# The first stage of a diffusion block rebuilt: modulation on column groups of TensorE, its squares summed there, and the values of two heads at a time

## The chip, the cores and the metric

One core of one Trainium2 chip. The metric is device time in microseconds (us), the median of three runs of the whole program. The core has five engines that run side by side, each in the order of its own program: TensorE (PE in the rows; PEld is its weight load), VectorE (DVE), ScalarE (ACT), GpSimd (POOL) and SyncE (SP), which here mostly issues transfers. Semaphores order one engine after another.

## The reference, cut to what matters

One block of a diffusion backbone, on 128 context tokens and 1024 latent tokens of 1024 features. What the change touches is the very beginning:

```
sh1, sc1, ... = silu(cond) @ w_mod + b_mod            # cond: one vector for the context, one for the sample
h   = x * rsqrt(mean(x*x) + eps) * g_norm_mix * (1 + sc1) + sh1    # 1152 tokens x 1024 features
z   = h @ w_in                                        # latents, q, k, v (1024 columns), gates, branches
```

Behind it come an attention over compressed latents, a bidirectional mLSTM (4 heads, values of 256 columns a head), gates, an output projection and a feed-forward part. All products are done in float32 accuracy.

## The kernel before, in words

Tokens lie along the free dimension and features on the 128 partitions: x^T is 8 row blocks (k = 0 to 7) of 128 features by 1152 tokens, handled in two halves of 576 tokens. Each operand of a large product is split into a high part (`hi`, ScalarE, L69) and a low part (`lo`, VectorE, L75: the difference), and a product is three matmuls, L98 (hi, hi), L99 (hi, lo) and L100 (lo, hi).

`start` (L329) is the first stage. Its steps:

- Transfers, in the order of SyncE's queue: two blocks of the modulation's matrix (`wm`, 1 MB each), the first half of x (four transfers, 2.36 MB), the first weights of the values (`wr`, 0.5 MB), the second half of x, then four more `wm` blocks and further weights.
- `gemv(b)` (L354): four times 128 columns of the modulation. Eight matmuls with the condition (128 rows, 2 columns) on the weight side and 512 columns of w_mod on the moving side (L356), then four small matmuls that turn the two rows into columns (L361). It is called for b = 0, 1, 2. The last two feature blocks, k = 6 and 7, are done instead as rows against a broadcast condition (`row`, L375 to L386, weights `wm3`) on VectorE, GpSimd and ScalarE.
- `stats(j)`: ScalarE squares a row block of half j, VectorE adds it to an accumulator (`sq_acc`, L156). `rows` (L259) then sums the accumulator over the partitions by five fp32 matmuls against a column of ones (L267), VectorE does rsqrt on 5 columns (L117 to L123) and five diagonal matrices `dg` (L274), TensorE broadcasts (L280) and ScalarE copies the factors to `ar` (L281).
- `xr(j)` (L423) multiplies the row blocks by the factors, k = 0 and 1 on VectorE, 2 to 7 on GpSimd. `modk(k, j)` applies scale and shift (ScalarE for the first half, VectorE L428 for the second) and splits the result into the operands B (high and low).
- The values: one head at a time (N = 256), 9 token chunks in the groups GA (6 chunks) and GB (3 chunks), each with an own PSUM bank; 4 heads x 9 chunks x 8 k x 3 = 864 matmuls. Only head 0 of group GA is multiplied while the modulation runs. A weight block (`wr`, 128 x 1024, four k of a head) is split into `wh` and `wl`, which share four buffers. `copy4` (L442, GpSimd) collects the chunk that straddles both halves; `vout` copies a finished bank to `vs` and stores it.
- `t_ops` (L543): four subtractions of 128 x 2304 elements on GpSimd (L547 and the like) that prepare operands of later products. They run beside the values.

Behind `start` comes `z_lat` (L574), whose first product is the first matmul with 288 columns. The order is that of each engine's instructions, which a scheduler settles from the code; the waits come from the buffers and from the data.

Of the kernel before, what the change touches and what calls it, by code (L numbers as in the profile page):

```python
# [19 lines left out]
P = 128  # L20
# [36 lines left out]
class K:  # L57
# [25 lines left out]
    def load_w(self, src, kt, w, bufs=None):  # L83
        """Stream one weight block [P, kt, w] from DRAM and split it exactly."""
# [27 lines left out]
    def rsqrt(self, ssq, width, n, pool):  # L112
        """1/sqrt(ssq/n + eps) on the vector engine: exponent estimate and three Newton steps."""
# [12 lines left out]
    def row_rstd(self, rbc, acc, n, pool, pp, tag, chunks=CHUNKS, more=None):  # L126
        """rbc[:, t] = 1/sqrt(sum_p (acc[p, t] + more[p, t])/n + eps) on every partition."""
# [30 lines left out]
    def modulate(self, raw, t, sc, sh, k):  # L158
        """raw = t * sc + sh with the context's and the sample's own columns."""
# [4 lines left out]
    # ------------------------------------------------------------------  # L164
# [48 lines left out]
    # vec columns  # L213
    V_GMIX, V_GFFN, V_GFIN, V_GML, V_GQ, V_GKV, V_BG = 0, 8, 16, 24, 32, 35, 37
# [24 lines left out]
    def tick(self, n=1):  # L239
        """Emit n pieces of the work that runs beside the products."""  # L240
# [18 lines left out]
    def rows(self, rbc, acc, n, pool, pp, tag):  # L259
        """rbc[:, t] = 1/sqrt(sum_p acc[p, t]/n + eps) on every partition."""  # L260
# [28 lines left out]
    def inputs(self):  # L289
        """Everything that reads the modulated input (all of w_in), the mLSTM and the attention's projections."""  # L290
# [38 lines left out]
    def start(self, vp):  # L329
        """Norm and modulation of the input, and the mLSTM's values."""  # L330
        nc, a, pp = self.nc, self.a, self.pp
        es = contextlib.ExitStack()
        sp = es.enter_context(self.pool("s1"))
        nc.scalar.dma_start(self.silc, a["cT"])
# [12 lines left out]
        def block(b):  # L347
            for i in range(2):
                w = self.slot(((8, 9), (10, 11), (5, 6))[b][i], [P, 4, 512], "wm", F32)
# [18 lines left out]
        sr = self.slot(7, [P, 2, D], "sr0", F32)  # L368
        rw = {}

        def rload(f):
            rw[f] = self.wp.tile([P, D], F32, name=self.nm("wr"), tag="wr", bufs=self.wb[0])
            nc.sync.dma_start(rw[f], a["wm3"][f])

        def row(f):  # L375
            """Shift (f even) or scale of block 6 + f // 2 of the features, as rows against the broadcast condition."""
            w = rw.pop(f)
            m = 8 * (f % 2) + 6 + f // 2
            o = self.mod1[:, m]
            for e in range(2):  # L380
                if e == 0 or f in (2, 3):
                    t = sp.tile([P, D], F32, name=self.nm("mj"), tag="mj")
                    nc.vector.scalar_tensor_tensor(t, w, 1.0, sr[:, e], op0=ALU.mult, op1=ALU.mult, accum_out=o[:, e:e + 1])
                else:
                    nc.gpsimd.tensor_tensor(w, w, sr[:, 1], op=ALU.mult)
                    nc.scalar.activation(w, w, AF.Copy, accum_out=o[:, 1:2])  # L386

        def rparams(k):
            for m in (k, 8 + k):
                nc.vector.tensor_scalar(self.mod1[:, m], self.mod1[:, m], self.bm[:, m:m + 1], None, op0=ALU.add)  # L390
            nc.vector.tensor_scalar(self.A1[:, k, :], self.mod1[:, 8 + k, :], 1.0,
                                    self.vec[:, self.V_GMIX + k:self.V_GMIX + k + 1], op0=ALU.add, op1=ALU.mult)
        nc.scalar.activation(self.silc, self.silc, AF.Silu)
        ar = self.slot(13, [P, 2, T], "ar", F32)
        acc, rbc = ar[:, 0], ar[:, 1]
        wv, vraw = {}, {}

        def vload(i):
            vraw[i] = self.wp.tile([P, 4 * DV], F32, name=self.nm("wr"), tag="wr", bufs=self.wb[0])
            nc.sync.dma_start(vraw[i], a["w_v"][i // 2][:, i % 2 * 4 * DV:(i % 2 + 1) * 4 * DV])  # L400

        def loadv(h, j):
            i = 2 * h + j
            if i not in vraw:
                vload(i)
            if i and i + 1 < 2 * HM:
                vload(i + 1)
# [1644 lines left out]
```

## Time and profile before

| | us |
|---|---|
| runs | 2242.07, 2245.0, 2249.43 |
| median | 2245.0 |
| profiled execution, its span | 2242.8 |
| TensorE busy | 2083.1 (93%) |
| VectorE busy | 1659.5 (74%) |
| GpSimd busy | 1127.2 (50%) |
| ScalarE busy | 1068.0 (48%) |

The page gives no time of the profiled execution beside its span; the span is 2.2 us under the median of the runs. The TensorE clock in the page is the share of full speed that was granted (1.0 is 2.4 GHz, 0.5 is 1.2 GHz). The first of the 40 slices of the page (56 us each) shows TensorE at 6 tenths and the second at 7, all later ones at 8 or 9: the stage that is changed is where TensorE stands idle most.

### The profile page before, as it was taken

How to read it: one execution, taken by the hardware profiler on the slowest of the kernel's cores; microseconds unless marked ns; L12 is line 12 of the kernel's file. 1: busy time of each engine (PE TensorE's matmuls, PEld its weight loads, DVE VectorE, ACT ScalarE, POOL GpSimd, SP SyncE). 2: the span in 40 equal slices, each digit the busy share in tenths (PEclk: the TensorE clock that was granted, in tenths of full speed). 3: DMA queues.
4: the chain of work that ended last, by engine and by line, in shares of the span. 5: the costliest groups of instructions: out<-in, count | busy, mean ns of one | idle time of the engine just before them, and what ended most of it. 6: DMA issues, size and time to landing. Idle time of an engine off the chain costs nothing.

```text
span 2242.8 us, 40186 instructions
## 1 busy us (share of the span) xinstructions
PE 2083.1 (93%) x14713; PEld 1998.2 (89%) x14713; DVE 1659.5 (74%) x2998; ACT 1068.0 (48%) x2225; POOL 1127.2 (50%) x850
## 2 busy tenths in 40 slices
PE   6799999999989987999999999879999999989898
PEld 2799998999978776998998999879999999989897
DVE  6725745988845879998987666899755565799895
ACT  4322333445445556777776435444322222356464
POOL 3612122667624415877877543677867634431411
PEclk8899999999999998999999999999999999999899
DMA  7121244555479775322224575223555522557664
GB/s 286 63 93 59 90 142 124 164 174 183 152 241 330 238 230 175 90 74 65 84 66 102 170 224 157 86 83 122 186 177 183 175 89 80 161 173 248 206 201 138
DMA packets 234532, 340.97 MB, mean 152 GB/s; under 512 B 18110, under 2 KB 170398, under 8 KB 233310
## 3 DMA queue, kind: packets, MB, share of 16 engines
q1 hardware_dynamic: 225790, 328.73, 46.0%
q0 software_dynamic: 4848, 6.06, 1.1%
q10 hardware_dynamic: 3696, 3.61, 0.5%
q8 instruction: 116, 1.90, 0.4%
q14 instruction: 82, 0.67, 0.1%
HBM read 250.55 MB, written 87.80 MB: 151 GB/s over the span
## 4 chain that ended last, share of the span: by engine, by line
PE 42%; DVE 16%; DMA 7%; POOL 6%; issue 6%; ACT 2%; SPq 1%; DVEq 0%; POOLq 0%; ACTq 0%
PE mm L98 10%; PE mm L100 10%; PE mm L99 10%; DVE wo L75 4%; DMA pr<-w_fo 3%; DVE sm L1374 2%; DVE pl L75 1%; PE st L98 1%; PE pv L1437 1%; PE pv L1438 1%; PE st L100 1%; PE st L99 1%; PE mx L1372 1%; DMA N<-d_nm 1%; PE p L1079 1%
## 5 line engine op out<-in xcount | busy, mean ns | idle before, releaser
L100 PE MATMUL mm<-th,wo 128*128 128x288 f32 x1840 | 546.8, 298 | 14.0 <-DVE wo L75 13.7
L98 PE MATMUL mm<-th,wo 128*128 128x288 f32 x1840 | 547.6, 298 | 2.7 <-DVE zo L1658 1.1
L99 PE MATMUL mm<-tl,wo 128*128 128x288 f32 x1840 | 546.2, 297 | 0.0
L100 PEld LDWEIGHTS mm<-th,wo 128*128 128x128 f32 x1840 | 348.9, 190 | 18.2 <-DVE wo L75 17.6
L75 DVE TENSOR_TENSOR wo<-wr,wo 128x512 fp32r<-128x512 f32 (+1 forms) x317 | 314.6, 1008 | 59.4 <-ACT wo L69 54.4
L98 PEld LDWEIGHTS mm<-th,wo 128*128 128x128 f32 x1840 | 348.2, 189 | 4.5 <-issue 1.6
L99 PEld LDWEIGHTS mm<-tl,wo 128*128 128x128 f32 x1840 | 348.3, 189 | 0.1
L69 ACT ACTIVATE wo<-wr 128x512 fp32r<-128x512 f32 (+1 forms) x317 | 187.5, 607 | 147.9 <-PE mm L100 69.5
L69 ACT ACTIVATE wo<-ws 128x512 fp32r<-128x512 f32 x188 | 116.7, 627 | 271.7 <-PE mm L100 160.5
L75 DVE TENSOR_TENSOR wo<-ws,wo 128x512 fp32r<-128x512 f32 x188 | 186.7, 996 | 62.1 <-ACT wo L69 61.9
L100 PE MATMUL mm<-xh,wo 128*128 128x288 f32 x616 | 184.7, 301 | 10.3 <-DVE wo L75 10.3
L1642 POOL TENSOR_TENSOR ws<-wr,ws 128x512 f32<-128x512 f32 x47 | 62.3, 1326 | 243.5 <-DVE wo L75 238.2
L99 PE MATMUL mm<-xl,wo 128*128 128x288 f32 x616 | 184.7, 300 | 0.0
L98 PE MATMUL mm<-xh,wo 128*128 128x288 f32 x616 | 184.2, 299 | 0.5 <-ACT wo L69 0.5
L1420 POOL TENSOR_TENSOR es<-es,p 128x512 f32<-128x512 f32 (+1 forms) x96 | 129.4, 1348 | 34.8 <-ACT p L1403 19.9
L98 PE MATMUL mm<-B,wo 128*128 128x288 f32 x456 | 134.8, 296 | 2.6 <-DVE zo L1658 1.7
L100 PE MATMUL mm<-B,wo 128*128 128x288 f32 x456 | 134.8, 296 | 0.0
L99 PE MATMUL mm<-B,wo 128*128 128x288 f32 x456 | 134.8, 296 | 0.0
L701 POOL TENSOR_TENSOR wm<-wm,sr 128x512 f32<-128x512 f32 x64 | 100.1, 1567 | 65.2 <-DVE mj L700 49.2
L100 PEld LDWEIGHTS mm<-xh,wo 128*128 128x128 f32 x616 | 118.1, 192 | 12.7 <-DVE wo L75 12.5
L98 PEld LDWEIGHTS mm<-xh,wo 128*128 128x128 f32 x616 | 118.2, 192 | 0.7 <-ACT wo L69 0.7
L99 PEld LDWEIGHTS mm<-xl,wo 128*128 128x128 f32 x616 | 118.4, 192 | 0.0
(443 smaller groups left out, 6076.6 us busy)
## 6 DMA issues: line engine op xcount, KB each, us to landing
wr<-w_ff SPq DMA_DIRECT2D x56, 512.0 KB
wm<-wm SPq DMA_DIRECT2D x32, 512.0 KB
wr<-d_w SPq DMA_DIRECT2D x32, 512.0 KB
d_z<-zo SPq DMA_DIRECT2D x48, 288.0 KB
d_g<-uu SPq DMA_DIRECT2D x44, 288.0 KB
wr<-w_big SPq DMA_DIRECT2D x24, 512.0 KB
wr<-w_fo SPq DMA_DIRECT2D x24, 512.0 KB
pr<-w_fo SPq DMA_DIRECT2D x40, 256.0 KB
```

The source lines that it names most:

```text
L69: i = self.nc.scalar.activation(out, in_, AF.Copy)
L75: return self.nc.vector.tensor_sub(out, in_, f32v(hi)).ins
L98: mm(out, lhs[0], rhs[0], start=first, stop=False)
L99: mm(out, lhs[0], rhs[1], start=False, stop=False)
L100: self.pe = mm(out, lhs[1], rhs[0], start=False, stop=last).ins
L701: nc.gpsimd.tensor_tensor(w[:, n], w[:, n], sr[:, 1], op=ALU.mult)
L1079: self.pe = mm(p1, A[:, h], V[:, h], start=True, stop=not carried).ins
L1372: nc.tensor.matmul(s[:, :kc], q[0:QK, 0, q0 + t * P:q0 + (t + 1) * P], k[0:QK, 0, k0 + j * kc:k0 + (j + 1) * kc], start=True, stop=True)
L1374: nc.vector.tensor_reduce(sm[:, 3 * t + j:3 * t + j + 1], s[:, :kc], axis=AX.X, op=ALU.max, negate=True)
L1420: G.tensor_tensor(U["sum"][:, :m], U["sum"][:, :m], p[:, :m], op=ALU.add)
L1437: nc.tensor.matmul(pv[:, :n], v[:, i], ph[:, e, :n], start=c + e == 0, stop=False)
L1642: G.tensor_tensor(s4, a12, s2, op=ALU.subtract)
```

## The change

What it does, step by step:

- Transfers: x's first half is loaded ahead of the `wm` blocks; there are eight `wm` blocks (four gemvs) instead of six, and no `wm3`.
- `gemv(b)`: the condition is padded to 32 columns, and the eight matmuls write four groups of 32 PSUM partitions in turn (k modulo 4). ScalarE copies the whole bank, and the four small matmuls, now with a selector of two columns on the moving side (L366), add the groups up. All four b are done so.
- `stats(j)`: VectorE adds nothing. Each squared row block is summed at once by five fp32 matmuls with one column (L398), which accumulate over k in PSUM: 8 x 5 = 40 for each half.
- `modk`: for k = 0 to 3 VectorE does x times scale times factor in one instruction (L421) and ScalarE adds the shift (L422); for k = 4 to 7 GpSimd multiplies by the factor (L414) and ScalarE applies scale and shift (L424), in both halves.
- The values: two heads at a time, N = 512, so 432 matmuls. A weight block is now two k of a head pair, and group GB loads and splits the blocks again: 16 blocks instead of 8. The row blocks are used by all six chunks of GA as soon as they are modulated: k = 0 and 1 of the first half, then of the second, and from k = 2 on both halves of a row block. `vs` is 512 wide, and there are 18 stores instead of 36.

The diff, cut to its core:

```diff
         def gemv(b):
-            g = self.bank(pp, "mx")[0:2]
+            g = self.bank(pp, "mx")
             for k in range(KD):
-                nc.tensor.matmul(g, self.silc[:, k, :], gw[b, k // 4][:, k % 4], start=k == 0, stop=k == KD - 1)
-            rows = sp.tile([2, 512], F32, name=self.nm("rows"), tag="rows", bufs=2)
+                j = 32 * (k % 4)
+                nc.tensor.matmul(g[j:j + 32], sil[:, k], gw[b, k // 4][:, k % 4], start=k < 4, stop=k >= 4)
+            rows = sp.tile([P, 512], F32, name=self.nm("rows"), tag="rows")
             nc.scalar.copy(rows, g)
             pm = self.bank(pp, "mx")[:, 0:8].rearrange("p (f j) -> p f j", j=2)
             for f in range(4):
-                nc.tensor.matmul(pm[:, f, :], rows[:, f * P:(f + 1) * P], self.ident[0:2, 0:2], start=True, stop=True)
+                nc.tensor.matmul(pm[:, f, :], rows[:, f * P:(f + 1) * P], self.vec[:, self.V_SEL:self.V_SEL + 2], start=True, stop=True)
...
+        nc.scalar.activation(sil[:, :, 0:2], self.silc, AF.Silu)
+        order = [(hp, e, kk) for hp in range(2) for e in range(2) for kk in range(4)]
...
         def stats(j):
-            c = slice(j * GT, (j + 1) * GT)
+            st = self.bank(pp, "mm")
             for k in range(KD):
-                self.sq_acc(acc[:, c], xv(k, j), k == 0, sp, GT, "sq", 2)
-            for _ in self.rows(rbc[:, c], acc[:, c], D, sp, pp, "mm"):
-                pass
+                s = sp.tile([P, GT], F32, name=self.nm("sq"), tag="sq", bufs=2)
+                nc.scalar.activation(s, xv(k, j), AF.Square)
+                for i, c in enumerate(AT):
+                    nc.tensor.matmul(st[:, i:i + 1], s[:, c:c + P], self.ones[:, 0:1], start=k == 0 and i == 0, stop=k == KD - 1,
+                                     skip_group_check=True)
+            r = self.rsqrt(st[:, :5], 5, D, sp)
+            dg = sp.tile([P, 5, P], F32, name=self.nm("dg"), tag="dg")
...
+            for i0, n in ((0, 4), (4, 1)):
+                bc = self.bank(pp, "mm")
+                for i in range(i0, i0 + n):
+                    o = slice(i * P - AT[i], P)
+                    nc.tensor.matmul(bc[:, (i - i0) * P:(i - i0) * P + P - o.start], self.ones, dg[:, i, o], start=True, stop=True)
...
         def xr(j):
-            for k in range(KD):
-                eng = nc.vector if k in (0, 1) else nc.gpsimd
-                eng.tensor_tensor(xv(k, j), xv(k, j), rbc[:, j * GT:(j + 1) * GT], op=ALU.mult)
+            for k in range(4, KD):
+                nc.gpsimd.tensor_tensor(xv(k, j), xv(k, j), rbc[:, j * GT:(j + 1) * GT], op=ALU.mult)
         def modk(k, j):
             x = xv(k, j)
             for c, s in ((slice(0, TP), 0), (slice(TP, GT), 1)) if j == 0 else ((slice(0, GT), 1),):
-                if j:
-                    nc.vector.tensor_scalar(x[:, c], x[:, c], self.A1[:, k, s:s + 1], self.mod1[:, k, s:s + 1], op0=ALU.mult, op1=ALU.add)
+                A, sh = self.A1[:, k, s:s + 1], self.mod1[:, k, s:s + 1]
+                if k < 4:
+                    nc.vector.scalar_tensor_tensor(x[:, c], x[:, c], A, rbc[:, j * GT + c.start:j * GT + c.stop], op0=ALU.mult, op1=ALU.mult)
+                    nc.scalar.activation(x[:, c], x[:, c], AF.Identity, bias=sh)
                 else:
-                    nc.scalar.activation(x[:, c], x[:, c], AF.Identity, bias=self.mod1[:, k, s:s + 1], scale=self.A1[:, k, s:s + 1])
+                    nc.scalar.activation(x[:, c], x[:, c], AF.Identity, bias=sh, scale=A)
...
-        def vmm(h, c, k):
+        def vmm(w, c, k):
...
-            w = wv[h, k // 4]
-            self.mm3(ps[c][:, :DV], hc(k, c), (w[0][:, k % 4], w[1][:, k % 4]), k == 0, k == KD - 1)
+            self.mm3(ps[c], hc(k, c), (w[0][:, k % 2], w[1][:, k % 2]), k == 0, k == KD - 1)
...
-        def vk(g, k):
+        G = GA[:4], GA[4:]
+        def vk(i, k, g):
             for c in g:
-                vmm(0, c, k)
+                vmm(wv[i], c, k)
+        xload(0)
         block(0)
-        xload(0)
         vload(0)
         xload(1)
         block(1)
+        vload(1)
         block(2)
-        vload(1)
+        vload(2)
+        block(3)
+        vload(3)
+        stats(0)
         gemv(0)
-        stats(0)
         xr(0)
-        gemv(1)
-        loadv(0, 0)
+        loadv(0)
+        for k in range(2):
+            modk(k, 0)
+            vk(0, k, G[0])
         stats(1)
         xr(1)
-        for k in range(4):
-            modk(k, 0)
-            vk(G0, k)
-        gemv(2)
-        for k in range(4):
+        gemv(1)
+        for k in range(2):
             modk(k, 1)
-            vk(G1, k)
+            vk(0, k, G[1])
+        for i in range(1, 4):
+            loadv(i)
+            for k in (2 * i, 2 * i + 1):
+                for j in range(2):
+                    modk(k, j)
+                    vk(i, k, G[j])
+                if k == 2 * i and i < 3:
+                    gemv(i + 1)
+            vload(i + 3)
+        c4 = self.slot(13, [P, 2, KD, P], "c4")
         copy4(0)
...
         copy4(1)
...
-        for h in range(HM):
-            for grp in (GA, GB):
-                for k in range(KD):
-                    if h == 0 and grp is GA:
-                        continue
-                    for c in grp:
-                        vmm(h, c, k)
-                    if grp is GB and k in (3, 7) and h + 1 < HM:
-                        loadv(h + 1, k // 4)
-                    if h and grp is GA:
-                        with self.tc.issue_after(self.last[0]), self.tc.issue_after(self.last[1]):
...
+        loadv(4)
+        for c in GA:
+            vout(0, c)
+        for i in range(4, len(order)):
+            hp, e, kk = order[i]
+            vload(i + 3)
+            for k in (2 * kk, 2 * kk + 1):
+                vk(i, k, (GA, GB)[e])
+                if k % 2 == 0:
+                    loadv(i + 1)
+                with self.tc.issue_after(self.last[0]), self.tc.issue_after(self.last[1]):
+                    self.tick()
+            if kk == 3:
+                for c in (GA, GB)[e]:
+                    vout(hp, c)
```

What the change moves, on TensorE first, ahead of the first product of the values. In the names a number only tells buffers apart: `wm` is a block of w_mod, `mx` a bank of the modulation, `sq` a squared row block, `dg` the diagonal factors, `wh` and `wl` a split weight, `B` and `b12` the split operands. Before:

```order
L356 MATMUL mx_257<-wm_156,silc 2x512 x4
L280 MATMUL mm_233<-dg_230,ones 128x128 x2
L280 MATMUL mm_240<-dg_237,ones 128x128 x2
L280 MATMUL mm_246<-dg_244,ones 128x64
L267 MATMUL mm_303<-ones,ar_140 128x1 x2
L356 MATMUL mx_257<-wm_158,silc 2x512 x4
L267 MATMUL mm_303<-ones,ar_140 128x1 x3
L361 MATMUL mx_268<-ident,rows_266 128x2 x4
L356 MATMUL mx_421<-wm_160,silc 2x512 x4
L356 MATMUL mx_421<-wm_162,silc 2x512 x4
```

Now:

```order
L398 MATMUL mm_174<-ones,sq_224 128x1 x5
L366 MATMUL mx_272<-vec,rows_270 128x2 x4
L361 MATMUL mx_422<-wm_156,sil 32x512 x4
L361 MATMUL mx_422<-wm_158,sil 32x512 x4
L408 MATMUL mm_252<-dg_246,ones 128x128 x4
L408 MATMUL mm_258<-dg_246,ones 128x64
L366 MATMUL mx_433<-vec,rows_431 128x2 x4
L361 MATMUL mx_496<-wm_162,sil 32x512 x4
L361 MATMUL mx_496<-wm_164,sil 32x512 x4
L98 MATMUL mm_297<-wh_285,B_51_293 128x512
```

Before, five column sums of the accumulated squares (L267, `mm_303`) stand for the second half of x, and three gemvs and both halves' factors come ahead of the products. Now only the first half's factors (L408) and three gemvs do; the first product stands right behind the gemv of `wm_162` and `wm_164`.

TensorE again, behind the products of the first half with k = 3. Before, at the place where the second half's products begin, there are only products:

```order
L98 MATMUL mm_369<-wh_489,B_88_495 128x256
L99 MATMUL mm_369<-wl_490,B_88_495 128x256
L98 MATMUL mm_444<-wh_277,b12h 128x256
L99 MATMUL mm_444<-wl_278,b12h 128x256
L98 MATMUL mm_448<-wh_277,b12h 128x256
L99 MATMUL mm_448<-wl_278,b12h 128x256
L100 MATMUL mm_357<-wh_489,B_89_496 128x256
```

Now:

```order
L98 MATMUL mm_309<-wh_464,B_51_293 128x512
L99 MATMUL mm_309<-wl_465,B_51_293 128x512
L100 MATMUL mm_309<-wh_464,B_52_294 128x512
L398 MATMUL mm_331<-ones,sq_367 128x1 x5
L398 MATMUL mm_331<-ones,sq_374 128x1 x5
L361 MATMUL mx_579<-wm_168,sil 32x512 x4
L361 MATMUL mx_579<-wm_170,sil 32x512 x4
L398 MATMUL mm_331<-ones,sq_381 128x1 x5
L366 MATMUL mx_590<-vec,rows_588 128x2 x4
L408 MATMUL mm_409<-dg_403,ones 128x128 x4
L408 MATMUL mm_415<-dg_403,ones 128x64
L98 MATMUL mm_446<-wh_285,b12h 128x512
```

The sums of the second half's squares (L398, the last three of eight row blocks), the fourth gemv and the second half's factors (L408) now stand between the products of both halves; the earlier sums are strewn among the products ahead of this.

VectorE, where it works on the second half of x. Before, with the copies `vs` of finished banks behind:

```order
L75 TENSOR_TENSOR b12l<-x_16_135,b12h 128x576 x2
L428 TENSOR_SCALAR x_18_137<-x_18_137,A_70,mod_68 128x576 x2
L75 TENSOR_TENSOR b12l<-x_16_135,b12h 128x576
L75 TENSOR_TENSOR B_91_513<-x_18_137,B_90_512 128x576 x2
L75 TENSOR_TENSOR B_89_496<-x_17_136,B_88_495 128x576
L75 TENSOR_TENSOR B_91_513<-x_18_137,B_90_512 128x576 x2
L462 COPY vs_635<-mm_361 128x256
L462 COPY vs_641<-mm_369 128x256
L462 COPY vs_644<-mm_444 128x256
L75 TENSOR_TENSOR wl_692<-wr_487,wh_691 128x1024
```

Now, from the diagonal factors on:

```order
L403 TENSOR_SCALAR dg_403<-ident,y_389 128x128 x5
L75 TENSOR_TENSOR B_86_553<-x_17_139,B_85_552 128x576 x2
L421 SCALAR_TENSOR_TENSOR x_16_138<-x_16_138,A_70,rbc 128x576 x4
L75 TENSOR_TENSOR b12l<-x_16_138,b12h 128x576 x2
L75 TENSOR_TENSOR B_88_570<-x_18_140,B_87_569 128x576
L75 TENSOR_TENSOR b12l<-x_16_138,b12h 128x576 x2
L75 TENSOR_TENSOR B_88_570<-x_18_140,B_87_569 128x576
L75 TENSOR_TENSOR wl_547<-wr_166,wh_546 128x1024
L75 TENSOR_TENSOR B_88_570<-x_18_140,B_87_569 128x576 x2
L75 TENSOR_TENSOR wl_627<-wr_172,wh_626 128x1024
```

The split `wl` of the next weights stood behind all of the modulation and the copies; now the split `wl_547`, which the products of k = 4 read, stands between the differences (L75) of the second half, behind four of the new L421.

## Rows read from the trace of the kernel before

**Rows 1.** Windows by stage: stretch, length, busy (count) by engine, clock, DMA share, GB/s.
```profile
0.00:59.00 59.00, 37.77 (x112) 14.58 (x113) 39.38 (x81) 27.42 (x45) 18.57 (x15) 0.82 0.74 286
59.00:103.07 44.07, 30.62 (x213) 29.22 (x212) 38.03 (x33) 15.60 (x28) 39.05 (x18) 0.89 0.13 45
103.07:182.90 79.83, 79.83 (x655) 79.83 (x656) 20.40 (x23) 19.59 (x26) 6.05 (x3) 0.98 0.26 84
182.90:2242.80 2059.90, 1934.90 (x13739) 1874.61 (x13737) 1561.67 (x2863) 1005.35 (x2128) 1063.49 (x814) 0.97 0.49 153
```

**Rows 2.** TensorE, timeline: start, length, what, [idle before and its end].
```profile
59.01 0.56 PE L98 MATMUL mm<-wh,B 128*128 128x256 f32 x1
...
103.07 0.58 PE L99 MATMUL mm<-wl,B 128*128 128x256 f32 x1 [3.07 <-DVE wl L75]
...
182.90 0.30 PE L98 MATMUL mm<-B,wo 128*128 128x288 f32 x1
```

**Rows 3.** TensorE, timeline: first and last of 25, then of four.
```profile
160.10 0.28 PE L100 MATMUL mm<-wh,B 128*128 128x256 f32 x1
...
162.98 0.28 PE L100 MATMUL mm<-wh,b12l 128*128 128x256 f32 x1
...
1255.07 0.34 PE L98 MATMUL mm<-hm,wh 128*128 128x384 f32 x1
...
1255.60 0.33 PE L98 MATMUL mm<-hm,wh 128*128 128x384 f32 x1
```

**Rows 4.** TensorE, timeline of the first 35 us.
```profile
16.24 1.02 PE L361 MATMUL mx<-ident,rows 2*128 2x2 f32 x8 [0.87 <-ACT rows L358]
...
17.55 1.27 PE L267 MATMUL mm<-ones,ar 128*128 128x1 f32 x10 [0.30 <-DVE ar L156]
...
24.63 4.97 PE L356 MATMUL mx<-wm,silc 128*2 128x512 f32 x8 [5.80 <-DMA wm<-wm]
29.53 1.33 PE L280 MATMUL mm<-dg,ones 128*128 128x128 f32 x10
...
31.18 3.60 PE L356 MATMUL mx<-wm,silc 128*2 128x512 f32 x8
```

**Rows 5.** Windows of 10 us.
```profile
20.00:30.00 10.00, 5.37 (x12) 1.19 (x13) 6.64 (x21) 3.33 (x5) 0.00 (x0) 0.66 1.03 420
30.00:40.00 10.00, 7.86 (x36) 4.38 (x35) 6.93 (x7) 7.52 (x12) 8.70 (x5) 0.88 0.90 364
...
50.00:60.00 10.00, 5.25 (x22) 5.00 (x23) 8.98 (x27) 3.02 (x8) 1.30 (x2) 0.57 0.46 157
```

**Rows 6.** VectorE, ScalarE: timeline, end of the first half's factors.
```profile
25.65 0.17 DVE L123 SCALAR_TENSOR_TENSOR y<-t,y 128x5 f32<-128x5 f32 x1
...
25.92 1.07 DVE L274 TENSOR_SCALAR dg<-ident,y 128x128 f32<-128x128 f32 x5
...
30.28 0.93 ACT L281 COPY ar<-mm 128x256 f32<-128x256 f32 x3 [6.16 <-PE mm L280]
```

**Rows 7.** ScalarE, VectorE: timeline, second half's factors and modulation.
```profile
58.96 0.53 ACT L281 COPY ar<-mm 128x256 f32<-128x256 f32 x2 [2.58 <-PE mm L280]
...
72.61 5.33 DVE L428 TENSOR_SCALAR x<-x,A,mod 128x576 f32<-128x576 f32 x1
...
82.19 8.96 DVE L75 TENSOR_TENSOR B<-x,B 128x576 fp32r<-128x576 f32 x5
```

**Rows 8.** GpSimd, VectorE: timeline around 100 us.
```profile
96.82 5.11 POOL L547 TENSOR_TENSOR t<-x,x 128x2304 f32<-128x2304 f32 x1
...
98.11 4.90 DVE L75 TENSOR_TENSOR wl<-wr,wh 128x1024 fp32r<-128x1024 f32 x1 [5.97 <-ACT wh L69]
```

**Rows 9.** Groups by line, 0 to 186 us: shapes, count, busy, mean ns, idle.
```profile
L423 POOL TENSOR_TENSOR x<-x,ar 128x576 f32<-128x576 f32 x12 | 21.8, 1848 | 38.6 <-ACT ar L281 38.6
...
L156 DVE TENSOR_TENSOR ar<-ar,sq 128x576 f32<-128x576 f32 x14 | 10.6, 757 | 12.3 <-ACT sq L155 11.7
...
L69 ACT ACTIVATE wh<-wr 128x1024 fp32r<-128x1024 f32 x8 | 8.4, 1054 | 19.1 <-PE mm L99 19.1
```

More of the change, by code (lines that the diff above doesn't have):

```diff
@@ L333, in start @@
         sp = es.enter_context(self.pool("s1"))
+        sil = sp.tile([P, KD, 32], F32, name="sil")
+        rbc = sp.tile([P, T], F32, name="rbc")
+        nc.gpsimd.memset(sil, 0.0)
         nc.scalar.dma_start(self.silc, a["cT"])
@@ L367, in gemv @@
                                         self.vec[:, self.V_GMIX + k:self.V_GMIX + k + 1], op0=ALU.add, op1=ALU.mult)
[L368 to L395, printed above, removed]
@@ L396, in start @@
-        wv, vraw = {}, {}
-        def vload(i):
[L399 to L407, printed above, removed]
-            w = [self.wp.tile([P, 4 * DV], R32, name=self.nm(n), tag="wo", bufs=self.wb[1]) for n in ("wh", "wl")]
-            r = vraw.pop(i)
-            self.last = self.hi(w[0], r), self.lo(w[1], r, w[0])
-            wv[h, j] = [t.rearrange("p (k f) -> p k f", k=4) for t in w]
+        nc.scalar.activation(sil[:, :, 0:2], self.silc, AF.Silu)
@@ new lines, in start, with loadv @@
+        order = [(hp, e, kk) for hp in range(2) for e in range(2) for kk in range(4)]
+        raw, wv = {}, {}
+        def vload(i):
+            if i < len(order):
+                hp, _, kk = order[i]
+                raw[i] = self.wp.tile([P, 4 * DV], F32, name=self.nm("wr"), tag="wr", bufs=self.wb[0])
+                nc.sync.dma_start(raw[i], a["w_v"][hp][:, kk * 4 * DV:(kk + 1) * 4 * DV])
+        def loadv(i):
+            if i < len(order):
+                w = [self.wp.tile([P, 4 * DV], R32, name=self.nm(n), tag="wo", bufs=self.wb[1]) for n in ("wh", "wl")]
+                r = raw.pop(i)
+                self.last = self.hi(w[0], r), self.lo(w[1], r, w[0])
+                wv[i] = [t.rearrange("p (k f) -> p k f", k=2) for t in w]
@@ L413, in stats @@
+        AT = (0, P, 2 * P, 3 * P, GT - P)
         def stats(j):
-            c = slice(j * GT, (j + 1) * GT)
+            st = self.bank(pp, "mm")
             for k in range(KD):
-                self.sq_acc(acc[:, c], xv(k, j), k == 0, sp, GT, "sq", 2)
-            for _ in self.rows(rbc[:, c], acc[:, c], D, sp, pp, "mm"):
-                pass
+                s = sp.tile([P, GT], F32, name=self.nm("sq"), tag="sq", bufs=2)
[5 more added lines that the diff above has]
+            dg = sp.tile([P, 5, P], F32, name=self.nm("dg"), tag="dg")
+            for i in range(5):
+                nc.vector.tensor_scalar(dg[:, i, :], self.ident, r[:, i:i + 1], None, op0=ALU.mult)
+            for i0, n in ((0, 4), (4, 1)):
[3 more added lines that the diff above has]
+                    nc.tensor.matmul(bc[:, (i - i0) * P:(i - i0) * P + P - o.start], self.ones, dg[:, i, o], start=True, stop=True)
+                w = min(n * P, GT - i0 * P)
+                nc.scalar.copy(rbc[:, j * GT + i0 * P:j * GT + i0 * P + w], bc[:, :w])
@@ L436, in modk @@
             self.lo(l[:, k % 4], x, h[:, k % 4])
-        c4 = self.slot(13, [P, 2, KD, P], "c4")
+        c4 = None
         def copy4(i):
@@ L1956, in layout @@
     d["wm1"] = np.stack([np.concatenate([wm[:, c:c + 256], wm[:, D + c:D + c + 256]], 1).reshape(2, 4, P, 512)
-                         .transpose(0, 2, 1, 3).reshape(2, P, 2048) for c in range(0, 768, 256)])
-    d["wm3"] = np.stack([wm[:, c:c + P].T for k in range(6, KD) for c in (k * P, D + k * P)])
+                         .transpose(0, 2, 1, 3).reshape(2, P, 2048) for c in range(0, D, 256)])
     d["wm2"] = wm[:, 2048:].T.reshape(32, P, D)
@@ L1965, in layout @@
         vec[:, off:off + v.size // P] = v.reshape(-1, P).T
+    vec[:, 39:41] = np.arange(P)[:, None] % 32 == np.arange(2)
     bg = g["b_gates"][0]
@@ L1987, in layout @@
     d["w_sp"] = tiles(sp)[0]
[L1988 removed]
+    d["w_q"], d["w_k"], d["w_v"] = tiles(mq), tiles(mk), tiles(mv, 2 * DV)
     d["w_zq"], d["w_zkv"] = tiles(zq), tiles(zkv)
```

41 lines of the change are left out of this document (7 added, 34 removed).

## The prediction

> **What bounds the kernel now.** I read the windows by stage first. The stage that is changed ends at 182.90 us of 2242.8, where the first product of `z_lat` starts [rows 1, 2]. TensorE is busy 37.77 of the first 59.00 us, 30.62 of the next 44.07, and all of the last 79.83 [rows 1]; behind 182.90 it goes on with 1934.90 busy of 2059.90. So the end of this stage is what the change can move, and whatever it moves shifts all the rest, whose order on TensorE is the same but for neighbours that swap in the attention.
>
> The TensorE timeline then shows why it stands idle. The first product of the values starts at 59.01 [rows 2], when the second half's factors are written too (58.96 + 0.53 = 59.49) [rows 7]: nearly all products wait for VectorE, which is busy 39.38 of those 59.00 us [rows 1], with sums of squares and the rows of the modulation. From 59 to 103 the modulation holds TensorE back: a 2304-wide subtraction of GpSimd (5.11 us) and a 1024-wide split of VectorE (4.90) overlap [rows 8], and the split is what ends TensorE's wait of 3.07 at 103.07 [rows 2]. Five differences of VectorE take 8.96 together at 82.19, one scale and shift 5.33 at 72.61 [rows 7], against 0.757 for a 576-wide VectorE instruction early on [rows 9].
>
> **The products themselves.** At full speed a 256-column matmul follows the one before by (162.98 - 160.10)/24 = 0.120 us, a 384-column one by (1255.60 - 1255.07)/3 = 0.177 [rows 3]. A line through both gives 0.177 + 0.057 = 0.234 for 512, twice the 256-column one gives 0.240 as the upper end, and I take 0.227, as far below, as the lower. 864 x 0.120 = 103.7 us become 432 x 0.234 = 101.1: only 2.6 less. The rest of the gain has to come from an earlier start.
>
> **When the first product starts.** The bytes ahead of the third `wm` block are the same in both queues (2.1 + 2.36 + 0.5 + 2.36 + 1.05 MB), so it lands at 24.6 as before [rows 4]. Behind it come a `wm` block, a weight, and two `wm` blocks at 420, then 364 GB/s [rows 5]: 27.1, 28.4, 30.9 and 33.8 us. Of the first half's factors, the broadcast stands behind the second gemv, which needs the block of 27.1, and ScalarE's copy behind the split of the weight that lands at 28.4 (1.05 us [rows 9]); that gives about 32, as before, where the copy ended at 30.28 + 0.93 = 31.2 [rows 6]. The first product also stands behind the third gemv, whose second half (four matmuls) starts at 33.8. Four 512-column fp32 matmuls of two condition columns took 3.60 [rows 4] (eight records, two a matmul): 0.9 each, and the half a gemv 3.6. If the four column groups run side by side it is 0.9. I take the middle, 2.25: first product at 36.0, against 59.0.
>
> **From there to the second half's factors.** In TensorE's order between the first product and the last sum of squares stand 48 products (48 x 0.234 = 11.2), eight sets of five column sums (five took 1.27 [rows 4], so 10.2), four small matmuls of the modulation (1.02 [rows 4]) and the fourth gemv (1.8 if the groups run together, 7.2 if in series; I take the middle, 4.5). Sum 26.9. The clock was 0.66 at 20 to 30 us, where a half gemv took 4.97 instead of 3.60 [rows 4, 5], and I add that difference, 1.4, for a low clock at the start: 64.3. ScalarE's squares I cost at nothing: they run while TensorE does the products. Then rsqrt, 12 instructions at 0.17 to 0.27 from start to start (0.22: 2.6), five diagonals 1.07, broadcast 1.33, copies 0.93 [rows 4, 6]: 5.9, factors at 70.2, against 59.5 before. So the second half is modulated 11 us later than before, and this is the price of the change.
>
> **From the factors to the products of k = 4.** TensorE has 30 more products to do (24 with k = 0 to 3, six with the high weights of k = 4): 7.0 us. The next needs `wl_547`, which stands on VectorE behind four L421, and six differences, and takes 1024/576 of 0.757, 1.35 itself: 10 x 0.757 + 1.35 = 8.9. Beside it GpSimd does four multiplications, 1.85 each [rows 9], with which VectorE has so far taken turns (it fell behind by whole instructions in the rows above), 7.4, and then a 2304-wide subtraction, 5.11. Ends: 8.9, if nothing collides, and 8.9 + 7.4 + 2 x 5.11 = 26.5, if two subtractions come in front of the split. I take one, 21.4, since the rows of the same stretch before are full of such collisions: `wl_547` at 91.6. TensorE idles some 14 us there.
>
> **The rest.** 432 - 78 = 354 products behind it, 82.8 us: end of the stage at 174.4, against 182.9. The removed modulation of k = 6, 7 as rows, the sums on VectorE and 18 of 36 stores I cost at nothing of their own: they are in the start times above. The eight added splits (1.05 on ScalarE, 1.35 on VectorE) lie beside products: a block lasts 18 x 0.234 = 4.2 us or more, and both engines are a quarter busy in the stretch up to 182.90; the added 4.2 MB run where the queues are at 0.26 [rows 1]. If that cover fails once, as it did at 103.07, it costs some 3 us. Nor is it sure that such stalls go: the same subtractions and splits still meet.
>
> Sum: 174.4 - 182.9 = -8.5, on 2242.8: 2234.3. The profiled execution is 2.2 under the median of the runs, so 2236.5.
>
> A rule bears on the gemvs, in sentences apart: the Trainium skill (TensorE: Matmul & The Clock Gate, Part 3 on packing small matmuls in rows and columns) says that matmuls whose outputs lie at different groups of 32 partitions run at once, and gives 2.38 times the speed for three column groups. By it a gemv would take some 3.0 us (an estimate from 7.2 and that page), the factors would come 1.5 earlier, and the sum would be 2235. No row of before shows column groups.
>
> **Rivals.**
> - *Wider gain.* GpSimd and VectorE hardly meet: the subtraction waits for the last shift of k = 3, and the split may come first; the multiplications cost VectorE half their length. Then 8.9 + 3.7 = 12.6 in place of 21.4, and the end 8.8 earlier: -17.3, median 2227.7. For it: only four multiplications run on GpSimd instead of six. Against: the 8.96 and 5.33 [rows 7].
> - *Column groups in series.* The groups save nothing, so that the change doesn't do what it says. The half gemv costs 1.35 more, the fourth gemv 2.7: -8.5 + 4.1 = -4.4, 2240.6. For it: fp32 matmuls of two records each, and a moving side of 512 columns in each. Against: nothing in the rows.
> - *Slower: TensorE stays at 1.2 GHz while sums and products alternate.* From 50 to 60 us the granted clock was 0.57 with TensorE busy 5.25 of 10 [rows 5], and the stretch from the first product to the factors is small matmuls with waits in between. At 0.57 the 26.9 us become 47.2, less the 1.4 already counted: 19 later, end at 193.3, +10.4: 2255.4. It decides from 8.5 us added, where the gain is gone. Against: from 30 to 40 us, with 7.86 busy, the clock was 0.88.
>
> **How the numbers follow.** Likeliest 0.49: 2236.5, with an own range of 2230 to 2243 (pace of 512 columns 402 x 0.007 = 2.8, the gemv 2.7, one subtraction more or less 5.1). Wider gain 0.21, series 0.16, low clock 0.14. This kernel's measurement can tell some 0.3%, 6.7 us, from no change: faster is below 2238.3, slower above 2251.7. Of the likeliest about 0.7 falls below 2238.3, of the series case a fifth: 0.34 + 0.21 + 0.03 = 0.58 faster; slower 0.14, the rest 0.28. The range reaches into the wider gain with the fast gemvs (2227.7 - 4.1 - 2.8, about 2220) and most of the way to the low clock (2251).
>
> **What would show it.** First product near 36; last column sum near 64 and factors near 70; the wait ahead of the products of k = 4 ended by `wl_547` near 92; products 0.234 apart behind; `z_lat` from about 174. A gemv of 1.8 to 3 us shows column groups at work, one of 7 their absence. A granted clock under 0.7 from 36 to 64 shows the slow rival. The prediction is wrong if the factors come after 79, or if the products after `wl_547` wait for weight splits again and again, or if the stretch behind `z_lat`'s start, the same in both, isn't 2060 us within some 3.

## The result, and the profile after

The changed kernel took 2254.86 us (median of 9 runs, 2249.58 to 2256.84) against 2245.02 of the kernel before (9 runs, 2240.47 to 2249.43): ratio 1.0032, 95% interval 1.0019 to 1.0045. It is slower, by 9.8 us of the medians or 7.2 by the ratio, where 2236.5 was forecast. Its profiled execution has a span of 2254.4 us.

The stages come first, by the same view as [rows 1], but cut at the events that the prediction named: first product, end of the split `wl` of k = 4, first product of `z_lat`. (On the page of the kernel before, the 16th and the 27th slice show TensorE at 7 tenths as the second does, and not at 8 or 9; the first, at 6, is the lowest.)

```profile
0.00:42.20 42.20, 32.23 (x154) 22.73 (x154) 12.33 (x31) 16.02 (x25) 7.44 (x12) 0.98 0.98 384
42.20:96.76 54.56, 42.62 (x190) 33.55 (x191) 29.99 (x50) 27.54 (x46) 17.52 (x12) 0.66 0.01 4
96.76:180.31 83.55, 83.55 (x366) 69.06 (x365) 38.91 (x28) 28.08 (x28) 22.22 (x8) 0.99 0.41 135
180.31:2254.40 2074.09, 1942.62 (x13738) 1880.38 (x13736) 1559.23 (x2863) 1006.69 (x2129) 1059.50 (x814) 0.97 0.48 153
```

The first stage does end earlier, at 180.31 instead of 182.90 [rows 2]. But the work behind it takes 2074.09 us instead of 2059.90 [rows 1], 14.2 more in these two profiles. So there are two different misses: a gain of 2.6 instead of 8.5 in the stage, and a loss behind it where none was expected. The prediction had named the second as a sign of being wrong, if the work behind wasn't 2060 us within some 3.

TensorE's timeline in the stage (start, length; in brackets the idle time before and what ended it) answers to [rows 2 and 4]:

```profile
26.35 2.29 PE L398 MATMUL mm<-ones,sq 128*128 128x1 f32 x10
...
30.28 3.60 PE L361 MATMUL mx<-wm,sil 128*32 128x512 f32 x16
33.81 1.33 PE L408 MATMUL mm<-dg,ones 128*128 128x128 f32 x10
...
35.91 1.92 PE L361 MATMUL mx<-wm,sil 128*32 128x512 f32 x16
42.21 0.80 PE L98 MATMUL mm<-wh,B 128*128 128x512 f32 x1 [4.37 <-ACT B L69]
42.80 0.63 PE L99 MATMUL mm<-wl,B 128*128 128x512 f32 x1
43.23 0.63 PE L98 MATMUL mm<-wh,B 128*128 128x512 f32 x1
...
65.38 2.29 PE L398 MATMUL mm<-ones,sq 128*128 128x1 f32 x20
67.60 3.45 PE L361 MATMUL mx<-wm,sil 128*32 128x512 f32 x16
70.98 1.40 PE L398 MATMUL mm<-ones,sq 128*128 128x1 f32 x10
...
82.75 0.79 PE L98 MATMUL mm<-wh,b12h 128*128 128x512 f32 x1 [4.77 <-ACT b12h L69]
...
92.60 1.22 PE L100 MATMUL mm<-wh,b12l 128*128 128x512 f32 x2 [2.65 <-DVE b12l L75]
...
98.67 1.55 PE L98 MATMUL mm<-wh,B 128*128 128x512 f32 x6
100.06 0.39 PE L99 MATMUL mm<-wl,B 128*128 128x512 f32 x1
...
180.09 0.39 PE L100 MATMUL mm<-wh,c 128*128 128x512 f32 x1
180.31 0.29 PE L98 MATMUL mm<-B,wo 128*128 128x288 f32 x1
```

A modulation block of eight matmuls (16 records) takes 3.60 at 30.28 and 1.92 at 35.91, against 7.2 before: the column groups seem to run side by side, which the seventh experiment tests. Five column sums (10 records) take 2.29 at 26.35, and ten take the same 2.29 at 65.38: the first half's 40 sums ran at half speed. So did the first 21 products: 42.80 to 43.23 is a step of 0.43, and such steps go on to 53.9, against 0.227 behind 100.06.

The split `wl` of k = 4 is ready at 96.76 (next rows), but TensorE doesn't wait for it. It waits 2.65 for a difference of the second half (`b12l`), then goes on without a wait, at half speed up to 98.3, and comes to the first product with this `wl` at 100.06. The 354 products from there to 180.31 take 80.25 us.

The other engines at two places, as the first product nears and in the second half, which answer to [rows 7]; VectorE first, then GpSimd, then ScalarE:

```profile
35.63 5.25 DVE L421 SCALAR_TENSOR_TENSOR x<-x,A,rbc 128x128 f32<-128x128 f32 x4 [1.84 <-ACT rbc L410]
...
85.02 7.53 DVE L75 TENSOR_TENSOR b12l<-x,b12h 128x576 fp32r<-128x576 f32 x2
...
93.34 1.42 DVE L75 TENSOR_TENSOR b12l<-x,b12h 128x576 fp32r<-128x576 f32 x2
...
95.35 1.41 DVE L75 TENSOR_TENSOR wl<-wr,wh 128x1024 fp32r<-128x1024 f32 x1
...
35.79 4.60 POOL L414 TENSOR_TENSOR x<-x,rbc 128x576 f32<-128x576 f32 x3 [34.13 <-ACT rbc L410]
...
86.32 5.61 POOL L525 TENSOR_TENSOR t<-x,x 128x2304 f32<-128x2304 f32 x1
...
77.69 0.70 ACT L410 COPY rbc<-mm 128x512 f32<-128x512 f32 x2 [0.47 <-PE mm L408]
```

The first half's factors are there at 35.7, the second's at 78.39; `wl` of k = 4 at 96.76. Two differences at 85.02 take 7.53 beside a subtraction of GpSimd, where two take 1.42 at 93.34.

### The profile page after: what moved, and what is told of

It is laid out like the page before. It is cut to its first block, busy times and chain, and to the rows that moved or that the text cites. A ratio compares the mean times of both kernels' runs of the same rounds, so it can differ in the third digit from the quotient of the medians.

```text
span 2254.4 us, 39582 instructions
## 1 busy us (share of the span) xinstructions
PE 2101.0 (93%) x14445; PEld 2005.7 (89%) x14445; DVE 1640.5 (73%) x2970; ACT 1078.3 (48%) x2226; POOL 1106.7 (49%) x845
## 4 chain that ended last, share of the span: by engine, by line
PE 40%; DVE 17%; DMA 8%; issue 6%; POOL 6%; ACT 3%; SPq 1%; DVEq 0%; POOLq 0%; ACTq 0%
PE mm L98 10%; PE mm L100 10%; PE mm L99 10%; DVE wo L75 4%; DMA pr<-w_fo 3%; DVE sm L1352 2%; DVE pl L75 2%; PE pv L1416 1%; PE pv L1415 1%; PE p L1057 1%; DMA N<-d_nm 1%; PE st L98 1%; POOL ps L1707 1%; POOL ps L1710 1%; PE st L100 1%
## 5 line engine op out<-in xcount | busy, mean ns | idle before, releaser
L75 DVE TENSOR_TENSOR wo<-wr,wo 128x512 fp32r<-128x512 f32 (+1 forms) x317 | 313.4, 1005 | 56.1 <-ACT wo L69 53.1
L75 DVE TENSOR_TENSOR wo<-ws,wo 128x512 fp32r<-128x512 f32 x188 | 189.7, 1012 | 66.5 <-ACT wo L69 66.3
```

Of the source, the lines that this page charges most:

```text
L75: return self.nc.vector.tensor_sub(out, in_, f32v(hi)).ins
```

## The experiments

Ten kernels ran against the kernel before, two of them unchanged ones as controls. One landmark is used throughout: the start of the first 288-column product (end of the first stage). Two parts behind it matter, the attention (from the first scores for its maxima to its first output product) and all of TensorE's work behind the landmark (to the end of its last matmul, 7 to 8 us ahead of the end of the span).

**1 and 2, the order behind the stage.** The scheduler places instructions by times it computes itself, so a shift in the first stage changes the order in the attention. A few spare matmuls move these times, and with the right number the order becomes that of the other kernel. In the traces, another matmul stands at 1630 of TensorE's 13737 places behind the stage, all of them in the attention. (At 24 more places, right behind the stage, the order goes with the kernel and not with the spare matmuls.)

```diff
+            if k == 0 and c == 7 and w is wv.get(12):
+                for _ in range(4):
+                    nc.tensor.matmul(ps[c], hc(k, c)[0], w[0][:, 0], start=True, stop=True)
             self.mm3(ps[c], hc(k, c), ...)
```

> The changed kernel with four spare 512-column matmuls at the head of the last group's chain (their sums are overwritten), which shifts the scheduler's times so that behind the first stage the instructions of every engine stand in exactly the order of the kernel before. The first stage should end near 181.2 us (180.3 + 4 x 0.23). Theory A, the order behind the stage (it differs in the attention) costs the 12 us that the changed kernel loses there: median 2243 to 2247. Theory B, the loss behind the stage is not one of order (it comes from when the work starts, from the clock, or is scatter of the runs): median 2253 to 2258.

Measured: 2250.15 (the kernel before, run beside it, 2247.06), ratio 1.0017 (1.0003 to 1.0032), stage end 181.55, attention 389.4. The median lies between the two forecasts, so it doesn't decide alone. It is about 5 us under the changed kernel although 0.9 were added, and the attention is as short as that of before (392.5).

The mirror, 24 spare matmuls of 256 columns in the kernel before (the same edit with `h == 3`):

> The mirror image: the kernel before with 24 spare 256-column matmuls at the head of its last chain (24 x 0.12 = 2.9 us), which gives the work behind the stage exactly the order of the changed kernel. Theory A, order: 2245 + 2.9 + 12, median 2257 to 2262. Theory B, not order: 2246 to 2250.

Measured: 2265.10, ratio 1.0097 (1.0072 to 1.0121), stage end 186.5, attention 399.5. With the order of the changed kernel the kernel before becomes slow: 18 us, of which 3.6 lie in the stage with its spare matmuls. That is theory A, and more than its 2257 to 2262.

**3, column sums on TensorE or additions on VectorE.**

```diff
-                for i, c in enumerate(AT):
-                    nc.tensor.matmul(st[:, i:i + 1], s[:, c:c + P], self.ones[:, 0:1], ...)
+                self.sq_acc(acc, xv(k, j), k == 0, sp, GT, "sq", 2)
+            for i, c in enumerate(AT):
+                nc.tensor.matmul(st[:, i:i + 1], acc[:, c:c + P], self.ones[:, 0:1], start=i == 0, stop=True, ...)
...
```

> The changed kernel with the squares added on VectorE as before (8 additions of 0.76 us a half) and five column sums a half on TensorE in place of 40. Behind the stage the order is that of the kernel before. Theory 1, the 40 column sums are on the path to the second half's factors, TensorE spends some 10 us on them there: factors of the second half near 68 instead of 78.4, stage end near 172, and with theory A on the order a median near 2236, without it near 2247. Rival, VectorE takes the sums late and the path moves there: stage end not before 178.

Measured: 2226.78, ratio 0.9918 (0.9895 to 0.9940), stage end 164.0. This version is 0.8% faster than the kernel before. Of the 28 us to the changed kernel 16.3 are the stage (180.3 to 164.0); part of the rest is the order behind it, which is that of before. (The diagonal factors moved into the buffers of the squares, too.) The same landmarks in its trace, TensorE, then ScalarE, then VectorE and GpSimd:

```profile
13.79 2.26 PE L398 MATMUL mm<-ones,acc 128*128 128x1 f32 x10 [13.79 <-DVE acc L156]
...
30.96 0.79 PE L98 MATMUL mm<-wh,B 128*128 128x512 f32 x1 [9.05 <-ACT B L69]
...
40.54 1.17 PE L398 MATMUL mm<-ones,acc 128*128 128x1 f32 x10
...
79.50 0.79 PE L99 MATMUL mm<-wl,B 128*128 128x512 f32 x1 [3.73 <-DVE wl L75]
...
164.02 0.29 PE L98 MATMUL mm<-B,wo 128*128 128x288 f32 x1
...
50.51 0.70 ACT L412 COPY rbc<-mm 128x512 f32<-128x512 f32 x2 [0.19 <-PE mm L410]
...
74.09 5.36 DVE L75 TENSOR_TENSOR wl<-wr,wh 128x1024 fp32r<-128x1024 f32 x1 [1.93 <-ACT wh L69]
...
73.26 5.10 POOL L527 TENSOR_TENSOR x<-x,x 128x2304 f32<-128x2304 f32 x1 [0.63 <-ACT x L426]
```

The first product starts at 31.0 instead of 42.2, the sums of the second half end at 41.7 instead of 72.4, and its factors are there at 51.2 instead of 78.4. More than the expected 10 us, since the first half gains too: its sums are done at 16 instead of 28.6. Of the 27 us by which the factors come earlier, 7 are lost again ahead of the products of k = 4 and 4 behind. TensorE now does wait for `wl` there (3.73), whose split takes 5.36 beside a subtraction of GpSimd.

**4, TensorE kept busy in its waits.**

```diff
+                n = {0: 16, 5: 14}.get(c, 0) if w is wv[0] else 0
+                for i in range(n):
+                    nc.tensor.matmul(ps[c], zero.bitcast(R32), w[0][:, 0], start=i == 0, stop=False)
...
```

> The changed kernel with 16 spare matmuls (zero weights, they add nothing) ahead of the first product of the values and 14 ahead of the first product of the second half, in TensorE's waits. Theory 2, the low clock (0.427 us a product from 42 to 54 and from 83 to 99, against 0.228 at full speed) is what makes the first stage longer than forecast: products at full pace from the first on, second half's factors near 73 instead of 78.4, stage end near 174. Rival, the waits on VectorE set the end and the clock only fills them: stage end 178 to 181.

Measured: 2255.65, ratio 1.0047 (1.0027 to 1.0067), stage end 177.1, attention 397.1 (its order is not that of before). Between both: the first 24 products ran at full pace, but part of that was given back. The windows of 10 us (columns as in [rows 5]) show how:

```profile
50.00:60.00 10.00, 10.00 (x66) 9.00 (x65) 0.60 (x5) 5.16 (x10) 0.00 (x0) 1.00 0.00 1
60.00:70.00 10.00, 10.00 (x56) 7.41 (x55) 2.27 (x8) 2.38 (x4) 0.74 (x2) 0.60 0.00 1
70.00:80.00 10.00, 7.92 (x27) 6.66 (x27) 8.46 (x21) 5.12 (x10) 5.22 (x4) 0.55 0.01 2
```

From 60 to 70 TensorE is busy all the time, with column sums, a modulation block and the four small matmuls behind it, and the mean granted clock is 0.60 nevertheless. So the spare matmuls got back 3.2 us of the stage (180.3 to 177.1). What the low clock costs in all is not shown, since it was there again from 60 to 80.

**5, a control: the kernel before once more.**

> The kernel before, unchanged, as one more program: a control for the parts behind the first stage whose order is the same in all kernels (the mLSTM, 204.3 us in the first profile of before and 205 to 213 in others; the first part of the feed-forward, 529.9 against 531 to 538). Theory C, these parts scatter from one execution and one load of a program to the next: they differ by several us from the first profile of before here too, and the ratio lies within 0.3% of one. Rival, the changed first stage does something to them: here they stay within 2 us of 204.3 and 529.9.

Measured: 2244.85 against 2245.28, ratio 0.9997 (0.9983 to 1.0012); mLSTM 207.6, first part of the feed-forward 530.5. The ratio is that of theory C; the mLSTM moved by 3.3 us and the feed-forward by 0.6, so the scatter of single profiles is real in the first and not shown in the second.

**6, no multiplication on GpSimd.**

```diff
-            for k in range(4, KD):
-                nc.gpsimd.tensor_tensor(xv(k, j), xv(k, j), rbc[...], op=ALU.mult)
...
-                if k < 4:
+                if True:
                     nc.vector.scalar_tensor_tensor(x[:, c], x[:, c], A, rbc[...], ...)
```

> The changed kernel with the factors of k = 4 to 7 applied on VectorE as those of k = 0 to 3 are, so that GpSimd multiplies nothing in this stage but runs its subtractions; one spare matmul gives the work behind the stage the order of before on TensorE, GpSimd and SyncE. To be read against the changed kernel with the order of before (2250.2, stage end 181.6). Theory 3, GpSimd's multiplications hold up VectorE when the first product is due (5.25 us for four instructions at 35.6) and again behind the second half's factors: first product near 38.5 instead of 42.2, stage end near 175, some 6 us faster. Rival, VectorE's eight more instructions a half cost as much as the collisions: stage end 180 to 184.

Measured: 2241.85, ratio 0.9985 (0.9970 to 1.0000), stage end 180.07, first product at 38.9. The first half of theory 3 held, the second did not: eight of the combined multiplications of the second half (L420 in this kernel) now stand ahead of the differences on VectorE. TensorE's timeline, then VectorE's:

```profile
85.74 1.22 PE L100 MATMUL mm<-wh,b12l 128*128 128x512 f32 x2 [6.59 <-DVE b12l L75]
...
96.92 0.79 PE L99 MATMUL mm<-wl,B 128*128 128x512 f32 x1 [3.61 <-DVE wl L75]
...
35.75 1.80 DVE L420 SCALAR_TENSOR_TENSOR x<-x,A,rbc 128x128 f32<-128x128 f32 x4 [1.98 <-ACT rbc L410]
...
74.09 10.73 DVE L420 SCALAR_TENSOR_TENSOR x<-x,A,rbc 128x576 f32<-128x576 f32 x8 [1.31 <-ACT rbc L410]
```

Without GpSimd's multiplications beside them, the four instructions ahead of the first product take 1.80 instead of 5.25. The rival was right on the stage: what the collisions cost, the added instructions cost too. The stage ends 1.5 us ahead of that of the first experiment, and 0.7 of these are three spare matmuls fewer. The median is 8 us under; the kernel before, run beside both, was 1.8 lower too (2245.28 against 2247.06). What the rest is stays open.

**7, one column group.**

```diff
-            g = self.bank(pp, "mx")
-                nc.tensor.matmul(g[j:j + 32], sil[:, k], ..., start=k < 4, stop=k >= 4)
+            g = self.bank(pp, "mx")[0:32]
+                nc.tensor.matmul(g, sil[:, k], ..., start=k == 0, stop=k == KD - 1)
```

> The changed kernel with the eight matmuls of a modulation block in one column group, one after the other; seven spare matmuls (1.6 us) give the work behind the stage the order of before on TensorE, GpSimd and SyncE. To be read against the changed kernel with the order of before (2250.2, stage end 181.6). Theory 4, the column groups run side by side (a block took 1.9 us at full clock, 7.2 in the kernel before) and two blocks are on the path: a block takes 7 us, first product near 47, stage end near 192, median near 2260. Rival, transfers and VectorE hide it: stage end under 186.

Measured: 2255.02, ratio 1.0038 (1.0021 to 1.0055), stage end 190.1. Its third modulation block, in TensorE's timeline:

```profile
41.74 7.05 PE L360 MATMUL mx<-wm,sil 128*32 128x512 f32 x16
```

7.05 against 1.92 with four groups, 3.7 times. Against the first experiment, with 0.7 us fewer spare matmuls, the stage is 8.5 longer: the groups are worth some 8 us of the stage here. The median is only 4.9 above that of the first experiment, where theory 4 had 10.

**8, the sums on VectorE and no multiplication on GpSimd.**

> Squares added on VectorE and no multiplication on GpSimd, both edits together, with the order behind the stage as the scheduler makes it (neither that of before nor that of the changed kernel). With the sums on VectorE the stage ended at 164.0 and the median was 2226.8. Theory 3 carried over: the collisions are still there (4.08 us for four instructions at 26.1), stage end near 159, median 2219 to 2228 by the order. Rival, VectorE has too much to do then: stage end 164 to 168, median 2227 to 2235.

Measured: 2214.71, ratio 0.9870 (0.9844 to 0.9895), stage end 151.7, attention 389.8: the fastest version, 1.3% under the kernel before. With the sums on VectorE, removing GpSimd's multiplications is worth 12.3 us of the stage and 12.1 of the median, where it was worth less than 1 of the stage with the sums on TensorE.

**9, the order once more.** The kernel with the sums on VectorE, with 12 spare matmuls and so the order of the changed kernel behind the stage:

> The kernel with the sums on VectorE (stage end 164.0, attention 391.0 us, median 2226.8 with the order of before behind the stage), and 12 spare 512-column matmuls (2.7 us) at the head of its last chain, which give the work behind the stage the order of the changed kernel. Theory A, the order costs 12 to 14 us over the spare matmuls, of which some 7 in the attention: attention 396 to 400, median 2239 to 2245. Theory B, not order: attention 388 to 393, median 2228 to 2232.

Measured: 2237.10, ratio 0.9966 (0.9947 to 0.9984), stage end 167.4, attention 397.1. The attention is as theory A has it; the median is 10.3 over that of the order of before, 3.4 of it from the stage. That leaves 7 for the order, less than the 12 to 14 expected. The attention of both kernels, which differ by the spare matmuls of the first stage alone, first with the order of before, then with that of the changed kernel (window, busy time by engine):

```profile
830.20:1221.20 391.00, 362.70 (x2438) 339.81 (x2437) 348.15 (x679) 281.94 (x637) 290.71 (x230) 0.95 0.32 89
```

```profile
839.00:1236.10 397.10, 365.82 (x2439) 341.62 (x2438) 345.09 (x679) 282.14 (x637) 290.79 (x230) 0.94 0.32 88
```

Idle time of TensorE is 28.3 in the one and 31.3 in the other, and its busy time is 3.1 longer at a slightly lower clock. Its waits in the second and third eighth of the attention, in the one order and in the other (what waited, for what; total, times, longest):

```profile
PE pv L1417 <- DVE av L1447: 1.2, 1, 1.2
PE pv L1418 <- POOL pl L1387: 1.1, 2, 0.9
PE st L98 <- ACT q L1363: 0.4, 1, 0.4
```

```profile
PE mx L1355 <- DVE sm L1357: 2.2, 2, 1.2
PE st L98 <- ACT q L1366: 1.4, 3, 0.7
PE mx L1365 <- DVE sm L1357: 1.3, 1, 1.3
PE pv L1445 <- ACT dr L1442: 1.0, 2, 0.6
PE st L98 <- ACT p L1386: 0.7, 1, 0.7
PE pv L1420 <- ACT ph L69: 0.6, 1, 0.6
PE pv L1421 <- POOL pl L1390: 0.4, 1, 0.4
```

2.7 us against 7.6: in the order of the changed kernel TensorE waits here for the maxima of scores (`sm`) and for work of ScalarE. These are two eighths of the attention; over all of it the idle time differs by 3.0 only, so the other order waits less elsewhere. Why the busy time is longer is not shown.

**10, a control: the changed kernel once more.**

> The changed kernel once more, unchanged, as a control. Theory A: attention 396 to 400 us again (396.5 in its first profile), median 2252 to 2257, slower than before by 0.3 to 0.45%. Theory C, that its loss was scatter of one load of the program: attention 389 to 393, median within 0.2% of before.

Measured: 2257.67, ratio 1.0057 (1.0038 to 1.0077), stage end 180.8, attention 399.1. So the loss was not scatter of one load of the program.

Over all profiles with one of these two orders, the landmarks read in the same way (us):

| order behind the stage | kernels | attention | all TensorE work behind the stage |
|---|---|---|---|
| of before | before, again, 1, 3, 6, 7 | 392.5, 390.5, 389.4, 391.0, 387.9, 392.2 | 2052.7, 2056.1, 2060.7, 2058.9, 2056.3, 2058.1 |
| of the changed kernel | after, again, 2, 9 | 396.5, 399.1, 399.5, 397.1 | 2066.5, 2065.3, 2066.6, 2065.9 |

The two rows don't overlap: 390.6 against 398.1 on average in the attention, 2057.1 against 2066.1 behind the stage. So the order costs 9 us by the profiles. Shown are the 7.5 in the attention: outside it (the second column less the first) the rows do overlap, 1660.2 to 1671.3 against 1666.2 to 1670.0. When the attention starts doesn't decide: at 830.2 to 859.7 in the first row, at 839.0 to 852.5 in the second. The 14.2 of the first two profiles are more than the average because that of the kernel before is the shortest of its row. By the medians, less what the stage differs or the spare matmuls add, the order is worth 6 us (1 against the changed kernel), 14 (2 against the kernel before) and 7 (9 against 3). The fourth and the eighth kernel have orders of their own: attention 397.1 and 389.8, behind the stage 2070.6 and 2058.3.

## Why the prediction was wrong, by its own steps

- *"whatever it moves shifts all the rest, whose order on TensorE is the same but for neighbours that swap in the attention"*: this is the step that failed. The swaps were seen, and no cost was given to them. They cost 9 us by the profiles, 7.5 of them in the attention, shown both ways: the kernel before becomes slow with the order of the changed kernel, and the changed kernel is faster with that of before. 2.6 earlier and 9 later is +6.4; the ratio gives 7.2 (4 to 10 by the interval), the medians 9.8. What is between lies within what single profiles with one order differ by (8 us).
- *The stage as a sum*: it ended at 180.3 instead of 174.4. The first product came 6.2 late, the way from there to the factors took 2.0 more, the way on to the products of k = 4 0.3 more, and the products behind took 2.6 less: together 5.9.
- *The products*: 0.234 forecast, 0.227 measured, at the lower end of the range: 354 of them in 80.25 us against 82.8.
- *First product at 36.0*: it came at 42.2. TensorE's 32.23 busy us ahead of it are one stretch without a wait, from 5.6 to 37.8, so transfers were not what it waited for; the first half's 40 column sums, taken for granted in the sum, ran at half speed until 28.6 and pushed the second gemv and the factors to 35.7 instead of 32. The prediction had the third gemv as the last thing ahead of the first product and put the modulation of the first row blocks at nothing. The gemv was done at 37.8, and TensorE waited 4.37 more for the operand B: four L421 took 5.25 beside GpSimd's multiplications (without these the product came at 38.9). This collision was counted only for the second half.
- *From there to the second half's factors*: 34.2 forecast (36.0 to 70.2), 36.2 measured (42.2 to 78.4). Right in sum, though not in parts: the modulation block took 3.45 instead of 4.5, and 21 products at 0.43 lost some 4 us to the low clock, where 1.4 had been put down. What the term hid is that the sums need not be there at all: 16 us of the stage, by the third experiment.
- *From the factors to the products of k = 4*: 21.4 forecast, 21.7 measured (78.39 to 100.06). The number is right by luck. The wait was to be for `wl` on VectorE, some 14 us of it; `wl` was ready after 18.4, and TensorE didn't wait for it. It waited 9.6 in all (4.77 at 82.75, 2.20 at 87.03, 2.65 at 92.60) for operands of the second half. A subtraction of GpSimd did come in between, as forecast, but beside two of the differences, and the 24 products between and behind the waits ran at half speed.
- *Column groups in series*: refuted, 1.92 against 7.05. The Trainium skill's 2.38 for three groups (TensorE: Matmul & The Clock Gate, Part 3) points the same way; four groups of float32 matmuls gave 3.7 here. The sum of 2235 by the Trainium skill's figure took the fourth gemv alone; with the half of the third, 1.5 instead of 2.25, it would have been 0.75 less.
- *The slow rival, the low clock*: there (0.66 from first product to `wl`), but 3.2 us came back where it was taken away in part, not 19, and the stage still ended ahead of that of before; it isn't what made the kernel slower. That the rival's 2255.4 is so near the 2254.9 measured is chance. No rival had the order behind the stage, so the chance of slower, 0.14, had the wrong ground.

## What to carry to other kernels

Where a scheduler works from computed times, a change in one stage can reorder later ones: compare the order behind the change too, and before judging an edit, give both versions the same order by a few spare instructions. A sum over partitions is cheap on TensorE by the instruction, but 40 of them in a row stand in line with the products that follow; with the additions on VectorE instead, which was busy 12.3 of the first 42.2 us in the changed kernel, the stage was 16 us shorter. Two edits can be worth little apart and much together, as with GpSimd's multiplications here: less than 1 us of the stage alone, 12 with the sums moved. And a landmark that comes when it was forecast doesn't show that the forecast wait is there: ask the trace what ended the wait.

## What the runs showed of the hardware

- In the changed kernel the clock column read 1.00 from 10 to 30 us, while five column sums took 2.29 us, twice the 1.15 of later ones (ten in 2.29 at 65.38): in this stretch only the durations tell the clock.
- In the fourth experiment the mean granted clock from 60 to 70 us was 0.60, while TensorE was busy 10.00 of 10 us with column sums, a modulation block in column groups and small matmuls behind it.
- Eight float32 matmuls with 32 columns on the weight side took 1.92 us in four column groups (changed kernel) and 7.05 in one (seventh experiment), 3.7 times as long.
- VectorE's instructions took longer beside GpSimd's: four L421 5.25 us, against 1.80 in the sixth experiment, where GpSimd multiplied nothing; two differences 7.53 beside a subtraction, against 1.42 later in the same kernel.
